# Routing weights written by accumulating scatters, and an expert product with its operands swapped, in a one-core mixer and expert layer

## The chip, the cores and the metric

The kernel runs as one program on one of the eight cores of a Trainium2 chip. The metric is the device time of one execution in microseconds, the median of several executions. A core has five engines that run their own instruction streams in order and meet at semaphores: TensorE (PE; its weight loads are shown apart as PEld), VectorE (DVE), ScalarE (ACT), GpSimd (POOL) and SyncE (SP). DMAs are issued by SP, ACT and POOL and are moved by the core's 16 DMA engines.

## The reference, cut to what matters

320 tokens of width 2048 (256 of a prompt, 64 of a sample) go through a mixing layer and then through a product-key expert layer. The change is in the second:

```python
q = (xb @ w_query).reshape(tb, 8, 2, 128)
s = einsum('thpc,hpkc->thpk', q, sub_keys)          # 128 keys in each half
s1, i1 = top_k(s[:, :, 0], 16)
s2, i2 = top_k(s[:, :, 1], 16)
cand_s = s1[..., :, None] + s2[..., None, :]         # 256 candidates
top_s, top_j = top_k(cand_s, 16)                     # eidx = 128 * i1 + i2 of them
g = softmax(top_s)
a = gelu(einsum('td,thkd->thk', xb, expert_u[eidx]))
out = einsum('thk,thkd->td', g * a, expert_v[eidx])  # 16384 experts, 8 x 16 a token
```

So each token has 128 pairs of an expert number and a weight `g`. All is in float32.

## The kernel before, in words

**The stream.** All weights pass through one stream of halves. A half is 512 KB, a tile [128, 1024], loaded by SP into one of LA = 5 `raw` buffers. `split_one` makes of it two float32r tiles: ACT copies it to `hi`, DVE subtracts, `lo = raw - hi`. Four `hi` and four `lo` buffers stand ready, so that the split is at most four halves ahead of PE. For a half, PE runs 8 blocks of 3 matmuls (hi by hi, hi by lo, lo by hi), 24 in all.

**The order** is written by `Plan`, a model of the engines' clocks that runs while the kernel is built. Tasks are generators; `step()` between two blocks of PE's work lets each task emit its next instructions when the model's clock of PE has come to the time at which its inputs are ready. Costs in this model (`pe_cost`, `dve_cost`, `pool_cost`, and 1.05 for a gather on POOL) set where an instruction stands in its engine's queue. On the chip each engine then takes its queue in that order and waits for what is late.

**The stages.** The mixing layer and the query product use 280 halves. Then come 256 halves of `Up` (128 tiles of experts; one expert tile is two halves, and it gives `hs = gelu(x U)` for 128 experts and 256 prompt tokens) and 256 halves of `Down`. The prompt's tokens meet all 16384 experts densely; the weights `g` are put into a table `gd` in DRAM, 128 x 128 experts by 256 tokens, with zeros where a token did not pick the expert. The order of groups of 4 tiles (`GE = 4`): 24 groups of Up, which are 192 halves; then the first Down; after it 8 Up tiles and one Down in turn; Downs alone at the end. `NSPILL = 20` groups of `hs` go through DRAM (`hd`).

**The table of weights.** `route_lane` finds the top 16 on DVE, `decode(i)` turns the results of token tile i into expert numbers and weights and marks `("dec", i)`. When the three tiles are decoded, `weights_lane` runs 64 times `g_unit` for four tokens each: DVE writes two one-hot tiles `oa` and `ob` by comparing with a row of numbers, POOL multiplies `ob` by the high and the low part of the weights, PE multiplies `oa` by `ob` (4 matmuls of 256 columns), ACT copies the result from PSUM into `st`, DVE adds the low part to it, and each 16 tokens SP writes `st` to `gd`. When all 64 are done it marks `G`. Then `weights_in` loads `gg`, the weights of two groups; `weigh` multiplies `hs` by them tile by tile (`h4`, `g4`) and splits the product into `w`.

**Down.** The 128 x 128 blocks of expert_v (`hi`, `lo`) are PE's stationary operand, the 256 token columns of `w` move. The sum over 8 tiles is added to `x2`, which holds the residual with features on partitions, and the last of them goes out as `yT`.

**The sample's 64 tokens** do not go through the dense products. `gathers` has POOL gather their rows of expert_u (`pur`) and expert_v (`pvr`) by indirect DMA, 128 times 512 KB each, into NGS = 4 buffers `gs`; DVE takes a dot product with each row of the first (`dot`) and adds each row of the second by its weight (`axpy`).

Most instructions are recorded by a helper, so line 221 stands for all of them but the stream's matmuls (line 359); the tiles' names tell them apart.

Of the kernel before, what the change touches and what calls it, by code (L numbers as in the profile page):

```python
# [31 lines left out]
GE = 4  # L32
# [3 lines left out]
NGS = 4  # L36
HSN = 4
RATE = 380e3
# [4 lines left out]
TB = 16  # L43
LA = 5
SA = 3

# [34 lines left out]

class Task:
# [4 lines left out]
class Plan:  # L87
# [4 lines left out]
    def __init__(self):  # L92
        self.clk = {e: 0.0 for e in ("pe", "act", "dve", "pool", "dma")}
        self.task = self.main = Task(None)
        self.tasks = []
        self.done = {}
        self.uses = {}
        self.table = None

# [37 lines left out]
    def move(self, queue, out, src):  # L137

        at = max(self.last(out, True), self.last(src, False))
        if queue != "sync":  # L140
            at = self.clk[queue] = max(self.clk[queue], at) + (1.0 if queue == "pool" else 0.1)
        n = size(out) * out.shape[0] * 4
        self.clk["dma"] = max(self.clk["dma"], at) + n / RATE
        self.touch(out, self.clk["dma"] + 2.0, True)
        self.touch(src, self.clk["dma"] + 2.0, False)

    def gather(self, out, idx):
        at = self.clk["pool"] = max(self.clk["pool"], self.last(out, True), self.last(idx, False)) + 1.05
        self.clk["dma"] = max(self.clk["dma"], at) + size(out) * out.shape[0] * 4 / RATE
        self.touch(out, self.clk["dma"] + GLAT, True)  # L150
# [6 lines left out]
    def spawn(self, gen):  # L157
        self.tasks.append(Task(gen, self.task.at))
# [53 lines left out]
class Engine:  # L212
# [4 lines left out]
    def __getattr__(self, op):  # L217
        f = getattr(self.eng, op)

        def call(*a, **k):  # L220
# [4 lines left out]
            if op == "indirect_dma_start":  # L225
                p.gather(out, k["in_offset"].ap)
                return r
# [22 lines left out]
def dve_cost(op, a, k):  # L250
# [3 lines left out]
    return 0.07 + n / 0.96e3 * (6.2 if op == "reciprocal" else 1)  # L254
# [12 lines left out]
def hybrid_kernel(ctx: ExitStack, tc: tile.TileContext, ins, outs, stop=None):  # L267
# [20 lines left out]
    RAW = Slots(plan, stream, "raw", [128, 1024], F32, LA)  # L288
    HI = Slots(plan, stream, "hi", [128, 1024], F32R, SA + 1)
    LO = Slots(plan, stream, "lo", [128, 1024], F32R, SA + 1)  # L290
# [11 lines left out]
    pool.memset(one, 1.0)  # L302
    mhalf = consts.tile([128, 1], F32, name="mhalf")
# [5 lines left out]
    class Stream:  # L309
        def __init__(self):  # L310
            self.loads, self.halves = deque(), deque()

        def fetch(self):
            p, h = next(self.src, (None, 0))
            if p is None:
                return False
            raw = RAW.take()
            p.load(raw, h)
            self.loads.append((p, h, raw))
            return True  # L320

        def split_one(self):
            p, h, raw = self.loads.popleft()
            hi, lo = HI.take(), LO.take()
            act.activation(hi, raw, AF.Copy)
            dve.tensor_tensor(lo, raw, hi, op=ALU.subtract)
            RAW.give(raw)
            self.halves.append((p, h, hi, lo))

        def fill(self):  # L330
            while RAW.free and self.fetch():
                pass

        def ahead(self):
            self.fill()
            while HI.free and self.loads:
                if self.halves and plan.last(self.loads[0][2], False) > plan.now() + 1:
# [10 lines left out]
        def half(self):  # L348
            p, h, hi, lo = self.halves.popleft()
# [17 lines left out]
            HI.give(hi)  # L367
            LO.give(lo)
# [3 lines left out]
    class Piece:  # L372

        GAP = 0.0025
# [135 lines left out]

    s1 = ExitStack()
# [24 lines left out]
    def late_consts():  # L536
# [17 lines left out]
        dve.tensor_scalar(bgh, vec[:, V_BG:V_BG + 48], 0.5, None, op0=ALU.mult)  # L554

# [442 lines left out]
    spawn(late_consts())  # L998

# [131 lines left out]
    def open_route():  # L1131
# [5 lines left out]
        for n in ("iT0", "iT1", "wH", "wL"):  # L1137
            R[n] = p.tile([128, DN], F32R if n == "wH" else F32, name=n)
# [18 lines left out]
        spawn(weights_lane())  # L1157
# [19 lines left out]
    def rows_task():  # L1177
# [19 lines left out]
        dve.scalar_tensor_tensor(xs, x2s, r2[:, 3:4], xs, op0=ALU.mult, op1=ALU.mult)  # L1197

# [4 lines left out]
    def wq_in(h, p):  # L1203
        def go(ps):
# [9 lines left out]
            if p == 1:  # L1214
                plan.see(sk)
                yield
                for i in range(3):
# [66 lines left out]
    def weights_lane():  # L1284
        yield from need(*[("dec", i) for i in range(3)])
        rtmp.close()
        q = open_pool(gtmp, "gtmp")
        OA = Slots(plan, q, "oa", [128, 4, 128], F32R, 3)
        OB = Slots(plan, q, "ob", [128, 4, 2, 128], F32R, 3)
        ST = Slots(plan, q, "st", [128, 128, TB], F32, 2)  # L1290
        st = None
        for t0 in range(0, DN, 4):
            if t0 % TB == 0:
                st, = yield from take(ST)
            oa, ob = yield from take(OA, OB)
            spawn(g_unit(t0, oa, ob, OA, OB, ST, st))
        while len(gdone) < DN // 4:
            yield
        gtmp.close()
        open_late()  # L1300
        mark("G")

    gdone = []
    gd = dram.tile([DN // TB, 128, 132 * TB], F32, name="gd")
    hd = dram.tile([NG, 128, GE * DN], F32, name="hd")

    def decode(i):
# [37 lines left out]
        rows = slice(0, 128) if i < 2 else slice(64, 64 + DN - TP)  # L1345
        n = rows.stop - rows.start
        if n:
            bk, = yield from take(BK)
            for a, nm in enumerate(("i0", "i1", "wt")):
                pe.transpose(bk[:, a * 128:a * 128 + n], R[nm][rows, i].rearrange("p h k -> p (h k)"), ident[rows, rows])  # L1350
            yield
            c = slice(i * 128, i * 128 + n)
            for a, nm in enumerate(("iT0", "iT1", "wH")):
                act.activation(R[nm][:, c], bk[:, a * 128:a * 128 + n], AF.Copy)
            dve.tensor_tensor(R["wL"][:, c], bk[:, 256:256 + n], R["wH"][:, c], op=ALU.subtract)
            BK.give(bk)
# [24 lines left out]
    def g_unit(t0, oa, ob, OA, OB, ST, st):  # L1381

        io = cst[:, None, C_IO:C_IO + 128].to_broadcast([128, 4, 128])
        col = lambda nm: R[nm][:, t0:t0 + 4, None].to_broadcast([128, 4, 128])
# [4 lines left out]
        yield  # L1389
        b2 = yield from take(BK, BK)  # L1390
        for k in range(4):
            mm(b2[k // 2][:, (k % 2) * 256:(k % 2) * 256 + 256], oa[:, k, :], ob[:, k].rearrange("p j i -> p (j i)"),
               start=True, stop=True)
        OA.give(oa)
        OB.give(ob)
        yield
        o, work = t0 % TB, []
        for a, bk in enumerate(b2):
            v = bk.rearrange("p (t j i) -> p t j i", t=2, j=2)
            s2 = st[:, :, o + 2 * a:o + 2 * a + 2].rearrange("p i t -> p t i")  # L1400
            act.activation(s2, v[:, :, 0], AF.Copy)
            work.append((s2, v[:, :, 1], bk))
        yield
        for s2, x, bk in work:
            dve.tensor_tensor(s2, s2, x, op=ALU.add)
            BK.give(bk)
        if o == TB - 4:
            plan.see(st)
            yield
            sync.dma_start(gd[t0 // TB][:, :128 * TB], st.rearrange("p i t -> p (i t)"))  # L1410
            ST.give(st)
        gdone.append(t0)

# [3 lines left out]
    def open_experts():  # L1417
# [3 lines left out]
        X["GS"] = Slots(plan, p, "gs", [128, W], F32, NGS)  # L1421
        spawn(gathers())

    def open_late():
        p = open_pool(late, "late")
        X["WT"] = Slots(plan, p, "w", [128, 2, 2 * GE, DN], F32R, 2)
        X["GG"] = Slots(plan, p, "gg", [128, DN // TB, 2 * GE * TB], F32, 1)

    def gathers():

        yield from need(("dec", 2))
        for src, use in (("pur", dot), ("pvr", axpy)):
            for j in range(128):
# [3 lines left out]
                spawn(use(j, gs))  # L1437
# [28 lines left out]
    class Up(Piece):  # L1466
# [16 lines left out]
        def after(self, b):  # L1483
            if b == 15:
                spawn(up_in(self.e, self.ps))

# [29 lines left out]
    def weigh():  # L1516
        for g in ORDER:
# [5 lines left out]
            h4 = hs.rearrange("p e (b t) -> p e b t", t=TB)  # L1523
            g4 = gg.rearrange("p b (e t) -> p e b t", t=TB)
            for k in range(GE + 1):
                if k < GE:
                    dve.tensor_tensor(h4[:, k], h4[:, k], g4[:, o + k], op=ALU.mult)
                    act.activation(w[:, 0, o + k, :], hs[:, k, :], AF.Copy)
                if k:
                    dve.tensor_tensor(w[:, 1, o + k - 1, :], hs[:, k - 1, :], w[:, 0, o + k - 1, :], op=ALU.subtract)  # L1530
                yield 0
# [14 lines left out]
    class Down(Piece):  # L1546

        def __init__(self, q, c, last):
            self.q, self.c, self.final, self.src = q, c, last, ins["pv"][8 * q + c]

        def ready(self, h):
            return plan.has(("w", self.q)) and MM.ready(1, plan.now())

        def begin(self, h):
            self.ps = MM.take()

        def moved(self, b):
            w, e = w_of[self.q], b % 8
            return self.ps[:, :DN], w[:, 0, e, :], w[:, 1, e, :], e == 0, e == 7

        def after(self, b):
            if b % 8 == 7:
                k = 2 * self.c + b // 8
                dve.tensor_tensor(x2[:, k, :DN], x2[:, k, :DN], self.ps[:, :DN], op=ALU.add)
                MM.give(self.ps)
                if self.final:
                    sync.dma_start(outs["yT"][k], x2[:, k, :DN])
            if b == 15 and self.c == 7:
                X["WT"].give(w_of.pop(self.q))
# [170 lines left out]
```

## Time and profile before

| | |
|---|---|
| time, median of 3 runs | 2733.84 us (2730.56 to 2739.34) |
| the profiled execution | 2734.69 us, span 2732.9 us from the first to the last instruction |
| PE busy | 2633.5 us, 96% of the span |
| DVE, ACT, POOL busy | 2024.8, 1137.6, 941.2 us |
| mean granted clock of TensorE | 0.985 |
| moved by DMA | 626.31 MB, 229 GB/s over the span |

The profile is one execution. Busy time is a mean over stages with different limits, so the stages are read one by one; PE's clock is given as a share of 2.4 GHz.

### The profile page before, as it was taken

Reading aid. Unit: us, or ns where it says so; the run is one execution under the profiler, and the core shown is the slowest. Engines: PE = TensorE matmul, PEld = TensorE weight load, DVE = VectorE, ACT = ScalarE, POOL = GpSimd, SP = SyncE. Lnnn points to the kernel's source line nnn. Section 1 sums busy time; section 2 is a strip of 40 time slices with the busy share of each in tenths; the row PEclk is TensorE's granted clock in tenths of the full one; section 3 lists DMA queues with packets and bytes.
Section 4 is the critical chain, followed back from the end, with each engine's and each line's share of the span. In section 5 each row is a group of like instructions: output and inputs, shape, how many; then the busy total and the mean of one; then the engine's idle time right before and its main releaser. Section 6 shows DMA issues by size and latency. Waiting matters only on the chain. (4 is left out here: it accounts for less than half of the span.)

```text
span 2732.9 us, 49761 instructions
## 1 busy us (share of the span) xinstructions
PE 2633.5 (96%) x19824; PEld 2587.2 (95%) x19824; DVE 2024.8 (74%) x3201; ACT 1137.6 (42%) x1613; POOL 941.2 (34%) x728
## 2 busy tenths in 40 slices
PE   7999999999999999999889898999999999999998
PEld 5899989999999999999889898999999999999997
DVE  8545666344444449999999998888778888888887
ACT  4344444333333334344444444444444444344442
POOL 7423342000001222045878877422223321122122
PEclk9999999999999999999999999999999999999999
DMA  7433333444444554456777787798988888888887
GB/s 229 166 124 120 123 113 131 150 151 147 154 147 147 176 173 141 152 185 222 271 279 275 272 284 271 296 318 302 333 310 308 310 329 298 310 299 312 289 293 255
DMA packets 217560, 626.31 MB, mean 229 GB/s; under 512 B 19824, under 2 KB 74096, under 8 KB 215280
## 3 DMA queue, kind: packets, MB, share of 16 engines
q1 hardware_dynamic: 174944, 470.40, 49.1%
q0 software_dynamic: 39504, 142.24, 14.9%
q10 hardware_dynamic: 2880, 10.49, 1.0%
q8 instruction: 157, 2.57, 0.4%
q14 instruction: 75, 0.61, 0.1%
HBM read 589.36 MB, written 33.69 MB: 228 GB/s over the span
## 5 line engine op out<-in xcount | busy, mean ns | idle before, releaser
L221 DVE TENSOR_TENSOR lo<-raw,hi 128x1024 fp32r<-128x1024 f32 x792 | 1035.7, 1311 | 568.3 <-ACT hi L221 560.8
L221 ACT ACTIVATE hi<-raw 128x1024 fp32r<-128x1024 f32 x792 | 835.0, 1058 | 1106.1 <-PE mm L359 961.0
L359 PE MATMUL mm<-xb,hi 128*128 128x256 f32 x4096 | 758.6, 287 | 2.9 <-ACT hs L221 2.8
L359 PE MATMUL mm<-w,hi 128*128 128x256 f32 x4096 | 737.6, 283 | 0.0
L359 PEld LDWEIGHTS mm<-xb,hi 128*128 128x128 f32 x4096 | 654.4, 196 | 3.3 <-ACT hs L221 3.0
L359 PEld LDWEIGHTS mm<-w,hi 128*128 128x128 f32 x4096 | 639.0, 192 | 0.0
L359 PE MATMUL mm<-x_g,hi 128*128 128x320 f32 x2688 | 602.9, 313 | 0.0
L359 PE MATMUL mm<-xb,lo 128*128 128x256 f32 x2048 | 587.9, 287 | 0.8 <-DVE lo L221 0.8
L359 PE MATMUL mm<-w,lo 128*128 128x256 f32 x2048 | 579.6, 283 | 0.0
L359 PEld LDWEIGHTS mm<-x_g,hi 128*128 128x128 f32 x2688 | 447.2, 188 | 8.0 <-issue 3.9
L359 PE MATMUL mm<-x_g,lo 128*128 128x320 f32 x1344 | 415.7, 309 | 0.9 <-DVE lo L221 0.9
L359 PEld LDWEIGHTS mm<-xb,lo 128*128 128x128 f32 x2048 | 402.2, 196 | 1.3 <-DVE lo L221 1.2
L359 PEld LDWEIGHTS mm<-w,lo 128*128 128x128 f32 x2048 | 393.2, 192 | 0.0
L221 POOL DMA_INDIRECT gs<-pvr,idx x128 | 178.6, 1395 | 531.3 <-DVE x2s L221 525.4
L221 POOL DMA_INDIRECT gs<-pur,idx x128 | 188.9, 1476 | 223.0 <-DVE gs L221 199.6
L359 PEld LDWEIGHTS mm<-x_g,lo 128*128 128x128 f32 x1344 | 252.7, 188 | 1.2 <-DVE lo L221 1.2
L221 POOL TENSOR_TENSOR r<-r 128x320 f32<-128x320 f32 (+2 forms) x39 | 39.6, 1017 | 403.0 <-DVE r L221 398.4
L221 DVE SCALAR_TENSOR_TENSOR gs<-gs,xs 128x1024 f32<-128x1024 f32 x128 | 173.1, 1355 | 0.1
L221 DVE SCALAR_TENSOR_TENSOR x2s<-gs,act,x2s 128x1024 f32<-128x1024 f32 x128 | 163.7, 1279 | 1.8 <-DMA gs<-pvr,idx 1.5
L221 POOL TENSOR_TENSOR ob<-ob,wL 128x512 fp32r<-128x512 f32 x64 | 142.3, 2223 | 5.0
L221 DVE TENSOR_TENSOR r<-r,mm 128x256 f32<-128x256 f32 x256 | 106.3, 415 | 43.5 <-PE mm L359 43.4
L221 POOL TENSOR_TENSOR ob<-ob,wH 128x512 fp32r<-128x512 f32 x64 | 114.8, 1794 | 62.2 <-DVE ob L221 56.7
(246 smaller groups left out, 2730.3 us busy)
## 6 DMA issues: line engine op xcount, KB each, us to landing
raw<-pu SPq DMA_DIRECT2D x256, 512.0 KB
raw<-pv SPq DMA_DIRECT2D x256, 512.0 KB
raw<-win SPq DMA_DIRECT2D x168, 512.0 KB
raw<-wbr SPq DMA_DIRECT2D x32, 512.0 KB
raw<-wout SPq DMA_DIRECT2D x32, 512.0 KB
raw<-wq SPq DMA_DIRECT2D x32, 512.0 KB
gd<-st SPq DMA_DIRECT2D x16, 1024.0 KB
gg<-gd SPq DMA_DIRECT2D x16, 1024.0 KB
```

The source lines that it names most:

```text
L221: r = f(*a, **k)
L359: nc.tensor.matmul(o, stays, moves, start=first, stop=last and n == len(products) - 1)
```

## The change

**Weights.** The one-hot products, `g_unit`, `weights_lane`, their pool and the buffers `st` go. The table is now two DRAM tensors `gd[0]`, `gd[1]`, one for each 128 prompt tokens. A new task `clear` has ACT fill them with zeros early, 32 DMAs of 512 KB. `decode(i)` works out for each pair of token and choice the word's place in the table (`ga`) and its weight (`gw`); `scatters` has POOL issue, for each of the 128 choices and both token tiles, one indirect DMA that adds 128 single words (one for each token) to the table. The sixteen of a head and tile may be in flight together; the first of the next head waits until the sixteen before it in that tile have landed. When the last 32 are issued, `G` is marked, and the first load of `gg` waits for their landing. Token tiles are now scored in the order 2, 0, 1, so that the sample's tile is decoded first.

**Down.** `w` (128 of the tokens) is stationary, 512 features of expert_v move. A half of Down is now 1 MB, two `raw` slots, read as 2 KB pieces. The result has tokens on partitions, so the residual is turned first (`turn`: 32 transposes on PE into `x2t`) and the sum is turned back at the end (`home`: 32 transposes). The tile `r1`, free after `turn`, now holds the gather buffers, five of them.

**The rest.** `weigh` takes a group of 4 tiles by one instruction each (1024 elements instead of 256). `raw`, `hi`, `lo` are rings of which two neighbours can be taken at once (LA = 4; two more `raw` slots when the expert stage opens, four more `hi` and `lo` after the last Up). The planner's costs are other numbers, and it books DMAs by queue.

```diff
-TB = 16
-LA = 5
+LA = 4
 SA = 3
+AHEAD = 6.0
...
+    def scatter(self, idx, src):
+        at = self.clk["pool"] = max(self.clk["pool"], self.last(src, False), self.last(idx, False)) + 1.05
...
-    return max(0.107, n + 0.003) if op == "matmul" else 0.216
+    return max(0.107, n + 0.0133) if op == "matmul" else 0.216
...
-    return 0.07 + n / 0.96e3 * (6.2 if op == "reciprocal" else 1)
+    return 0.16 + n / 0.96e3 * (6.2 if op == "reciprocal" else 1)
...
+    def clear():
+        yield from need(("x",))
+        for q in range(NG // 2):
+            for g in gd:
+                act.dma_start(g[q].rearrange("p (a x) -> p a x", x=128), zeros[:, None, :].to_broadcast([128, 2 * GE, 128]))
+            at = plan.now() + 12.0
+            while plan.now() < at:
+                yield
...
-                for i in range(3):
+                for i in (2, 0, 1):
...
+    def scatters():
+        yield from need(*[("ga", i) for i in range(DN // 128)])
+        for h in range(8):
+            for k in range(16):
+                for i in range(DN // 128):
+                    own = rounds.setdefault((h, i), [])
+                    j = 16 * h + k
+                    r = pool.indirect_dma_start(
+                        out=gd[i].rearrange("q p (x o) -> (q p x) o", o=1),
+                        out_offset=bass.IndirectOffsetOnAxis(ap=R["ga"][:, i, j:j + 1], axis=0),
+                        in_=R["gw"][:, i, j:j + 1], in_offset=None, compute_op=ALU.add)
+                    earlier = rounds[h - 1, i] if k == 0 and h else []
+                    after(r, earlier)
...
+                yield 0
...
-    def g_unit(t0, oa, ob, OA, OB, ST, st):
...
-        dve.tensor_tensor(ob[:, :, 1, :], io, col("iT1"), op=ALU.is_equal)
-        pool.tensor_tensor(ob[:, :, 0, :], ob[:, :, 1, :], col("wH"), op=ALU.mult)
-        pool.tensor_tensor(ob[:, :, 1, :], ob[:, :, 1, :], col("wL"), op=ALU.mult)
-        dve.tensor_tensor(oa, io, col("iT0"), op=ALU.is_equal)
...
-            act.activation(s2, v[:, :, 0], AF.Copy)
...
-            dve.tensor_tensor(s2, s2, x, op=ALU.add)
...
-        X["GS"] = Slots(plan, p, "gs", [128, W], F32, NGS)
+        x2t.append(p.tile([128, DN // 128, 2048], F32, name="x2t"))
+        X["GS"] = Slots(plan, None, "", None, None, NGS)
+        X["GS"].make = lambda i: r1[:, W * i:W * i + W]
+        RAW.extend(p.tile([128, 2048], F32, name="raw2"))
...
-            sync.dma_start(gg, gd[:, :, GE * TB * g:GE * TB * (g + 2)].rearrange("b p e -> p b e"))
+            for i in range(DN // 128):
+                r = sync.dma_start(gg[:, i].rearrange("p e t -> p (e t)"), gd[i][g // 2])
+                if g == ORDER[0]:
+                    after(r, rounds[7, i])
...
+            dve.tensor_tensor(h4, h4, gg[:, :, o:o + GE].rearrange("p i e t -> p e i t"), op=ALU.mult)
+            yield
+            act.activation(wh, hw, AF.Copy)
+            yield
+            dve.tensor_tensor(wl, hw, wh, op=ALU.subtract)
...
+        def block(self, b, hi, lo):
+            w, e, t = w_of[self.q], b // 2, b % 2
+            wh, wl = (w[:, i, e, 128 * t:128 * t + 128] for i in range(2))
+            vh, vl = (x.rearrange("p (k e d) -> p e k d", k=4, e=GE)[:, e % GE] for x in (hi, lo))
+            return (self.sums[t].rearrange("p (k d) -> p k d", k=4), e == 2 * GE - 1,
+                    ((wh, vh, e == 0), (wh, vl, False), (wl, vh, False)))
...
+            dve.tensor_tensor(x2t[0][:, t, c], x2t[0][:, t, c], ps, op=ALU.add)
```

Two places of the built programs show how instructions moved. First POOL's queue from the first gather on, before: `gs` are the gather buffers, `ob` the one-hot tiles, `wH` and `wL` the weights.

```order
L221 DMA gs_12688<-pur,idx 128x1024
L221 TENSOR_TENSOR ob_12677<-ob_12677,wH 128x4x128
L221 TENSOR_TENSOR ob_12677<-ob_12677,wL 128x4x128
L221 TENSOR_TENSOR ob_12679<-ob_12679,wH 128x4x128
L221 TENSOR_TENSOR ob_12679<-ob_12679,wL 128x4x128
```

POOL's queue of the change, where the scatters begin (`gd_92` and `gd_93` are the two tables, `r_80` the gather buffers):

```order
L271 DMA r_80<-pur,idx 128x1024 x4
L271 COPY gw<-wt 128x128
L271 DMA r_80<-pur,idx 128x1024
L271 DMA gd_92<-gw,ga 2097152x1
L271 DMA gd_93<-gw,ga 2097152x1
```

The 128 pairs of multiplications are gone. In their place stand 256 scatters, which alternate between the tables; 17 gathers stand ahead of the first of them, 8 between them, and 103 of `pur` and all 128 of `pvr` behind the last.

Second DVE's queue around the first `weigh`. Before (`lo` are the splits of the stream, the instructions on `gs,dots` are `dot`, those on `hs` the first `weigh`):

```order
L221 TENSOR_TENSOR lo_18127<-raw_17955,hi_18126 128x1024
L221 TENSOR_TENSOR lo_18159<-raw_17990,hi_18158 128x1024
L221 SCALAR_TENSOR_TENSOR gs_18014,dots<-gs_18014,xs 128x1024
L221 TENSOR_TENSOR lo_18193<-raw_18023,hi_18192 128x1024
L221 TENSOR_TENSOR hs_17576<-hs_17576,gg_18038 128x256 x2
L221 TENSOR_TENSOR w_18244<-hs_17576,w_18244 128x256
```

DVE's queue of the change at the same task (`r_80,dots` is `dot`; in the whole program 449 splits stand ahead of the first `dot` shown here, and 349 ahead of the last input of the first scatter):

```order
L271 TENSOR_TENSOR lo<-raw,hi 128x1024 x3
L271 SCALAR_TENSOR_TENSOR r_80,dots<-r_80,xs 128x1024
L271 TENSOR_TENSOR lo<-raw,hi 128x1024
L271 SCALAR_TENSOR_TENSOR r_80,dots<-r_80,xs 128x1024 x2
L271 TENSOR_TENSOR lo<-raw_10066,hi 128x1024
L271 SCALAR_TENSOR_TENSOR r_80,dots<-r_80,xs 128x1024 x2
L271 TENSOR_TENSOR lo<-raw_10066,hi 128x1024
L271 TENSOR_TENSOR lo<-raw,hi 128x1024
L271 TENSOR_TENSOR hs_15432<-hs_15432,gg_15508 128x1024
```

The first `dot` shown uses the first gather that POOL issues after the last scatter. It stands 100 splits behind the start of the scatters, and all later splits stand behind it. The 8 dots whose gathers are issued between scatters stand among those 100 splits. The first `weigh` was 463 splits from the start and is 453.

On PE, a half of Down was 24 matmuls of 256 columns on 512 KB and is 24 of 512 columns on 1 MB; 128 such halves stand where 256 stood. In both programs 192 halves of Up stand ahead of the first Down, and 64 behind it; 45 of the 128 dots stand on DVE ahead of the first Down's split in the change, 83 behind it.

## Rows read from the trace of the kernel before

**Rows 1.** The page, the span in 40 equal slices: busy tenths of two engines and of the DMA engines.

```profile
PE   7999999999999999999889898999999999999998
DVE  8545666344444449999999998888778888888887
...
DMA  7433333444444554456777787798988888888887
```

**Rows 2.** Windows: stretch, length; busy us (xcount) of PE, PEld, DVE, ACT, POOL; PEclk, DMA, GB/s.

```profile
600.00:700.00 100.00, 100.00 (x684) 100.00 (x684) 47.28 (x56) 37.23 (x42) 7.03 (x8) 1.00 0.43 149
1129.00:1266.00 137.00, 132.08 (x1076) 131.60 (x1075) 127.31 (x293) 61.63 (x81) 44.67 (x28) 0.98 0.56 188
1266.00:1797.00 531.00, 484.13 (x3811) 477.68 (x3810) 489.64 (x588) 245.90 (x363) 395.53 (x212) 0.95 0.78 279
1797.00:2719.00 922.00, 922.00 (x7686) 922.00 (x7685) 754.64 (x1024) 383.87 (x467) 227.39 (x172) 1.00 0.86 307
1900.00:2000.00 100.00, 100.00 (x836) 100.00 (x835) 83.66 (x122) 41.96 (x51) 24.76 (x23) 1.00 0.88 317
```

**Rows 3.** Timeline of PE, first Up, first Down, last Down: start, us, matmul.

```profile
1129.06 0.41 PE L359 MATMUL mm<-xb,hi 128*128 128x256 f32 x2
...
1797.36 0.40 PE L359 MATMUL mm<-w,hi 128*128 128x256 f32 x2
...
2719.05 0.28 PE L359 MATMUL mm<-w,lo 128*128 128x256 f32 x1
```

**Rows 4.** Waits in 1266 to 1797: us in total, times, longest.

```profile
PEld bk L221 <- POOL ob L221: 33.6, 10, 5.1
```

**Rows 5.** Groups by form: count, busy us, mean ns, idle before and its releasers.

```profile
L221 POOL DMA_INDIRECT gs<-pur,idx x128 | 188.9, 1476 | 223.0 <-DVE gs L221 199.6 <-issue 9.0 <-DVE idx L221 7.6
...
L221 DVE SCALAR_TENSOR_TENSOR gs<-gs,xs 128x1024 f32<-128x1024 f32 x128 | 173.1, 1355 | 0.1
L221 DVE SCALAR_TENSOR_TENSOR x2s<-gs,act,x2s 128x1024 f32<-128x1024 f32 x128 | 163.7, 1279 | 1.8 <-DMA gs<-pvr,idx 1.5
...
L221 DVE TENSOR_TENSOR r<-r,mm 128x256 f32<-128x256 f32 x256 | 106.3, 415 | 43.5 <-PE mm L359 43.4
...
L221 DVE TENSOR_TENSOR hs<-hs,gg 128x256 f32<-128x256 f32 x128 | 51.8, 419 | 2.6 <-DMA gg<-gd 2.6
...
L221 PE MATMUL bk<-ob,oa 128*128 128x256 f32 x256 | 48.0, 309 | 46.0 <-POOL ob L221 31.4 <-DVE st L221 14.2
...
L221 DVE TENSOR_TENSOR r<-mm,rb_x 128x320 f32<-128x320 f32 x56 | 27.1, 484 | 0.0
...
L221 PE MATMUL bk<-cst,r 128*128 128x128 f32 x20 | 2.8, 273 | 0.0
```

**Rows 6.** Timeline of POOL, gathers one behind the other: start, us.

```profile
2014.63 0.95 POOL L221 DMA_INDIRECT gs<-pvr,idx  x1 [0.30 <-issue]
2015.89 0.95 POOL L221 DMA_INDIRECT gs<-pvr,idx  x1 [0.30 <-issue]
2017.14 0.95 POOL L221 DMA_INDIRECT gs<-pvr,idx  x1 [0.30 <-DVE r L221]
```

**Rows 7.** Timeline of DVE over the same stretch.

```profile
2014.74 1.23 DVE L221 TENSOR_TENSOR lo<-raw,hi 128x1024 fp32r<-128x1024 f32 x1 [0.55 <-ACT hi L221]
...
2017.62 1.23 DVE L221 TENSOR_TENSOR lo<-raw,hi 128x1024 fp32r<-128x1024 f32 x1 [0.55 <-ACT hi L221]
```

**Rows 8.** Timeline of POOL, gathers while DVE is full.

```profile
1315.64 1.94 POOL L221 DMA_INDIRECT gs<-pur,idx  x1 [0.30 <-issue]
1317.89 0.95 POOL L221 DMA_INDIRECT gs<-pur,idx  x1 [0.30 <-issue]
```

**Rows 9.** The tile kT, a direct DMA of 128 rows issued by POOL: ns min/median/max.

```profile
L221 POOL DMA_DIRECT2D kT<-qk x8: 551/598/648, 228.5 to 441.4; - x8
```

**Rows 10.** Timeline of all engines at the end: the last gather and its use.

```profile
2721.25 1.87 POOL L221 DMA_INDIRECT gs<-pvr,idx  x1 [4.81 <-DVE x2s L221]
...
2726.49 1.28 DVE L221 SCALAR_TENSOR_TENSOR x2s<-gs,act,x2s 128x1024 f32<-128x1024 f32 x1 [1.55 <-DMA gs<-pvr,idx]
```

More of the change, by code (lines that the diff above doesn't have):

```diff
@@ L79, in give, with __init__, extend, left @@
         self.free.sort()
+class Ring:
+    def __init__(self, plan, tile_, n):
+        self.plan = plan
+        self.at = [tile_[:, i, :] for i in range(n)]
+        self.both = [tile_[:, i:i + 2, :].rearrange("p s c -> p (s c)") for i in range(n - 1)] + [None]
+        self.slots = Slots(plan, None, "", None, None, n)
+        self.slots.make = lambda i: self.at[i]
+    def extend(self, *pairs):
+        for x in pairs:
+            self.slots.free += [(self.plan.now(), len(self.at) + i) for i in range(2)]
+            self.at += [x[:, :1024], x[:, 1024:]]
+            self.both += [x, None]
+        self.slots.free.sort()
+    def left(self):
+        return len(self.slots.free)
+    def take(self, n):
+        at = sorted(i for t, i in self.slots.free[:n])
+        assert at[-1] - at[0] == n - 1
+        parts = [self.slots.take() for _ in range(n)]
+        return self.both[at[0]] if n == 2 else parts[0], parts
+    def give(self, parts):
+        for x in parts:
+            self.slots.give(x)
 class Task:
@@ L225, in call @@
             if op == "indirect_dma_start":
-                p.gather(out, k["in_offset"].ap)
+                if k["in_offset"] is None:
+                    p.scatter(k["out_offset"].ap, k["in_"])
+                else:
+                    p.gather(out, k["in_offset"].ap)
                 return r
@@ L335, in ahead @@
             self.fill()
-            while HI.free and self.loads:
-                if self.halves and plan.last(self.loads[0][2], False) > plan.now() + 1:
+            while self.loads and HI.left() >= self.loads[0][0].SLOTS:
+                if self.halves and max(plan.last(self.loads[0][2], False), plan.clk["dve"] - AHEAD) > plan.now() + 1:
                     break
@@ L508, in row_norm @@
         yield
+    gd = [dram.tile([NG // 2, 128, 2 * GE * 128], F32, name=f"gd{i}") for i in range(DN // 128)]
     s1 = ExitStack()
@@ L1282, in route_lane, with late_lane, after @@
                     spawn(decode(i))
-    def weights_lane():
+    def late_lane():
         yield from need(*[("dec", i) for i in range(3)])
         rtmp.close()
[L1287 to L1297, printed above, removed]
+        open_late()
+    rounds = {}
+    def scatters():
[11 more added lines that the diff above has]
+                    after(r, earlier)
+                    tc.declare_no_dep(r.ins, group=f"tile{i}", reason="other words", keep=[x.ins for x in earlier])
+                    own.append(r)
+                    tc.add_to_no_dep_group(f"tile{i}", r.ins)
+                yield 0
+        at = plan.clk["pool"] + 5.0
+        while plan.now() < at:
             yield
-        gtmp.close()
-        open_late()
         mark("G")
-    gdone = []
-    gd = dram.tile([DN // TB, 128, 132 * TB], F32, name="gd")
+    def after(r, others):
+        for x in others:
+            tc.add_manual_dep(r.ins, x.ins.name, mybir.DependencyInfo(mybir.DependencyClass.Sync, mybir.DependencyReason.DATA),
+                              reason="adds to the same words")
     hd = dram.tile([NG, 128, GE * DN], F32, name="hd")
@@ L1546, in hybrid_kernel, with load @@
     class Down(Piece):
+        SLOTS = 2
         def __init__(self, q, c, last):
-            self.q, self.c, self.final, self.src = q, c, last, ins["pv"][8 * q + c]
+            self.q, self.c, self.final = q, c, last
+        def load(self, raw, h):
+            n = 8 * self.q + 2 * self.c
+            sync.dma_start(raw.rearrange("p (k x) -> p k x", k=4),
+                           ins["pv"][n:n + 2, :, :, 512 * h:512 * h + 512].rearrange("n k p x -> p (n k) x"))
         def ready(self, h):
-            return plan.has(("w", self.q)) and MM.ready(1, plan.now())
+            return plan.has(("w", self.q)) and (h == 1 or MM.ready(2, plan.now()))
@@ L1554, in begin @@
         def begin(self, h):
[L1555 to L1559, printed above, removed]
-        def after(self, b):
[L1562 to L1565, printed above, removed]
-                if self.final:
-                    sync.dma_start(outs["yT"][k], x2[:, k, :DN])
-            if b == 15 and self.c == 7:
-                X["WT"].give(w_of.pop(self.q))
+            if h == 0:
+                self.sums = [MM.take(), MM.take()]
@@ L1575, in down @@
     def down(q, last=False):
-        for c in range(8):
+        for c in range(4):
             yield Down(q, c, last)
```

191 lines of the change are left out of this document (114 added, 77 removed).

## The prediction

> **What bounds the kernel now.** I read the page's slices first, then TensorE by stage, then the waits of the one stage where it is not full, then single instructions.
>
> The slices [rows 1] show PE at nine tenths or more nearly everywhere; the eights stand in the second half of the route and of the table of weights, and there DVE is full too. The stages [rows 2] put figures to it. From 1900 to 2000 us PE does 836 matmuls of 256 columns in 100 us, 119.6 ns each, at full granted clock; from 600 to 700 it does 684 of 320 columns, 146.2 ns each. The difference, 26.6 ns for 64 columns, is 0.416 ns a column, which is the 2.4 GHz level; what is left, 119.6 - 256 x 0.416 = 13.1 ns, is a price for each matmul. From 1797 to 2719 the same pace holds with DVE busy 754.6 of 922 us: this stage is bound by PE alone. From 1266 to 1797, where the table of weights is made, 3811 matmuls at 119.6 ns would take 455.8 us and took 531: 75.2 us are lost, with DVE busy 489.6 us of 531 and the granted clock at 0.95 instead of 1.00. What PE waits for there is the chain of `g_unit`, POOL's products first of all [rows 4]. From 1129 to 1266 (1076 matmuls, 128.7 us of work) 8.3 us are lost with DVE at 93%.
>
> First Up at 1129.06, first Down at 1797.36, last matmul at 2719.05 [rows 3]; the span ends 13.9 us later. I sum against the profiled execution, 2734.7 us, which lies 0.9 us above the median.
>
> **The change, part by part.**
>
> *Fewer matmuls.* The 256 of `g_unit` [rows 5] go: 256 x 119.6 ns = -30.6 us. Down does 3072 matmuls of 512 columns instead of 6144 of 256. No row has a pace for 512 columns; by the two above it is 119.6 + 256 x 0.416 = 226 ns, so 694.3 us instead of 734.8: -40.5 us. The bounds are 2 x 119.6 ns (nothing gained) and 213 ns (no fixed price, 40 us more); the line through two lengths is the nearest. The Trainium skill, TensorE: Matmul & The Clock Gate, section Back-to-back issue gap, has a fixed part of only 2.5 ns, which would make 215.8 ns and the sum 31 us lower; by the same rule 256 columns would take 109 ns, and the rows here say 119.6, so the trace decides.
>
> *The stall of the old table.* Its DVE work (two one-hot tiles, two sums), its POOL products and its PSUM copies go, and with them what waited: -75.2 us. Whether something new waits there comes next.
>
> *New on PE:* 64 transposes of 128 x 128. Nearest is the 273 ns of a 128-column matmul in float32 [rows 5], a latency and so an upper bound; +16 us (0 to 17).
>
> *The route's end.* The decodes of tiles 0 and 1 and 17 dots now stand between splits 328 and 349 of the stream. That DVE work (21 splits, 12 of the dots, 13 comparisons and reductions, some small ones: about 64 us with 1.23 us for a split, a comparison or a reduction, 1.355 for a dot [rows 5, 7] and 0.25, an estimate, for each small one) meets 60 us of PE: +5 us.
>
> *The scatters.* No row shows one. All 256 stand in POOL's queue between the last input `ga` (349 splits done) and the gather for the dot behind split 449. At PE's pace 100 splits are 100 x 24 x 119.6 ns = 287 us. In that time POOL must issue 256 scatters and 9 gathers. The planner that wrote the order booked 1.05 us for each. Gathers issued one behind the other start 1.25 to 1.26 us apart, 0.95 us of work and 0.30 us of issue [rows 6], and that with a split on DVE each 2.88 us [rows 7], which is just the load that DVE has beside the scatters. So 265 x 1.26 = 334 us. The first scatter of each head waits for the landing of the last of the head before; the last gather of all was in use 3.4 us after its issue ended [rows 10], less one scatter issued meanwhile, 2.1 us, seven times: 15 us. Then the landing of the gather that the dot wants, 3.4 us: 352 in all, 65 us more than PE needs. What is queued behind: the dot stands in DVE's queue ahead of all later splits, so DVE stops, `lo` tiles run out after at most three halves (8.6 us), and PE stops. The eight dots among the 100 splits spread this stop over the stage. So 65 - 8.6 = +57 us. SP's first `gg` waits for the same landings, with the later `raw` loads behind it; it is late together with DVE and costs nothing more.
>
> The bounds: a direct DMA of 128 rows takes POOL 0.60 us [rows 9], with 0.30 of issue 0.9 us each, and the stop is 0. With DVE full, gathers start 2.25 us apart [rows 8]: 265 x 0.99 = 262 us more, +319. I take 1.26 us, because instruction and DVE's load are nearest there; a scatter builds 128 addresses as a gather does. That the words are added in DRAM has no row; it lies behind POOL's issue and shows only in the waits between heads.
>
> The Trainium skill bears on the price, SBUF — State Buffer, section Who interferes with whom: a DVE instruction with two inputs from SBUF shuts out a GpSimd instruction that reads SBUF until it is done. Each split has two such inputs. The rows agree where DVE is full and not where it only splits; by the rule alone each scatter that meets a split would lose up to 1 us, and the sum would go toward the first rival below.
>
> *Down's margin.* After the first Down DVE has 64 splits at 1.23 us, 128 of double length (2.3 us, by 0.42 us at 256 elements and 1.23 at 1024), 83 dots at 1.355, 128 axpys at 1.279, 56 long instructions of `weigh` at 1.23 (before, 0.42 each at a quarter of the length), 128 sums of 512 columns at 0.69 us (by 0.415 at 256 and 0.484 at 320) [rows 5, 7]: 805 us beside 878 us of PE, 92%. DVE at 82% cost PE nothing and at 93% 6% [rows 2]. Downs have only two pairs of `hi` and `lo` until the Ups end, so one pair is made while the other is used, 5.4 us. Bounds 0 and 53 us; +18, since the 93% stand in a stage of short chained instructions.
>
> *Hidden.* The zeros are written early by DMAs from ACT's queue, where the DMA engines are three to four tenths busy [rows 1]; uncovered, 16.8 MB at 307 GB/s [rows 2] would be 55 us. The loads of expert_v come in 2 KB pieces, at a DMA share of 0.86 [rows 2]; Down's data per column are unchanged.
>
> The sum: 2734.7 - 30.6 - 40.5 - 75.2 + 16 + 5 + 57 + 18 = **2685 us**, 1.8% below the median.
>
> **The rivals.**
>
> *A: scatters cost more than 1.45 us (slower).* Place: POOL between splits 349 and 449. Each 0.1 us is 26.5 us, so the 49 us that the forecast gains are gone at 1.45 us. The mean gather of `pur`, 1.476 us [rows 5], with 0.30 of issue is 1.78: 265 x 0.52 = 138 more, 2823 us. For it: DVE's splits do meet POOL, and the addition in DRAM may want more addresses or land late. Against it: [rows 6, 7]; while DVE waits for a dot it does not disturb POOL.
>
> *B: scatters at the planner's pace or below (1.05 us or less).* Less data than a gather of 4 KB rows; the direct DMA speaks for it. The stop vanishes: 2685 - 57 = 2628 us.
>
> *C: 512 columns gain nothing*, if the fixed price grows with length: 2725 us. For it: no row at 512. Against: 256 and 320 lie on the 2.4 GHz slope.
>
> *D: DVE becomes the bound in Down* as from 1129 to 1266: 53 instead of 18 us, 2720 us. For it: 92%. Against: 82% cost nothing for 922 us.
>
> **How the numbers follow.** Forecast 0.40 (own range 2660 to 2715), B 0.20, C and D together 0.12, A 0.28. A measurement here tells 0.3% (8 us) from no change. Faster: the forecast, B, and half of C and D, 0.66; within 0.3%: the edge between C, D and A, 0.07; slower: A less that edge, 0.27. For 8 in 10 the range reaches from 2615 (B with a little of the stalls gone) to 2785 (half of A); above it lies 0.13, below it 0.06.
>
> **What would show it.** Matmuls of Down 226 ns apart; 24 of them in 5.4 us. Scatters starting about 1.26 us apart, with seven waits of a few us for DMA at the heads. Between first scatter and first `gg` DVE idle for gathers, PE idle for `lo`, some 57 us in all, and the granted clock below 1.00. The first Down at about 1129 + 551 + 5 + 57 + 10 = 1752 us instead of 1797. After it PE near 98%. Wrong: a scatter period far from 1.26 us, a gap at the heads near 10 us, or PE starved in Down.

## The result, and the profile after

The changed kernel takes 2899.41 us (median of 4 runs, 2897.74 to 2903.01) where the kernel before took 2736.59 us beside it: a ratio of 1.0599, 95% interval 1.0576 to 1.0623. It is 6% slower; 2685 us had been forecast. The profiled execution is one of 2899.26 us.

The page's slices, for the rows of [rows 1] and two more:

```profile
PE   7899999999999999999555725469999999999999
DVE  8446664444445578898122212158888888888895
POOL 6323330000002220157888888853444343333330
PEclk9899999999999999999777967779999999999999
DMA  7666433444444545568555545389999998999984
```

From slice 20 to 26, PE is half empty, DVE nearly idle, and POOL at eight tenths. Nothing else in the program looks worse than before. The stages, as in [rows 2]:

```profile
1129.00:1344.00 215.00, 208.29 (x1716) 206.89 (x1716) 192.49 (x473) 97.08 (x123) 77.53 (x53) 0.99 0.64 222
1344.00:1898.70 554.70, 307.02 (x2421) 305.18 (x2420) 134.10 (x126) 121.13 (x153) 468.72 (x264) 0.78 0.52 117
1945.00:2480.00 535.00, 534.42 (x3169) 472.15 (x3169) 442.83 (x442) 211.51 (x184) 204.69 (x138) 1.00 0.94 343
2480.00:2897.00 417.00, 407.18 (x1744) 326.48 (x1743) 337.71 (x256) 152.47 (x94) 125.61 (x77) 0.99 0.84 309
2700.00:2800.00 100.00, 100.00 (x431) 80.49 (x430) 84.20 (x67) 35.92 (x22) 34.55 (x23) 1.00 0.94 351
```

The second row is the stage of the scatters: 2421 matmuls of 119.6 ns are 289.6 us of work, and it lasts 554.7 us. Of the 265 us between, 17 are matmuls at a lower granted clock (0.78 in this stage, 307.0 us busy), the others idle time. Its waits (engine, line, waited for: us in all, times, longest) and the groups of the two instructions concerned, for [rows 4, 5]:

```profile
DVE r L271 <- DMA r<-pur,idx: 247.9, 8, 76.3
PEld mm L416 <- DVE lo L271: 196.5, 8, 69.4
PE mm L416 <- DVE lo L271: 194.8, 8, 69.2
...
POOL gd L271 <- issue: 77.0, 250, 1.1
POOL gd L271 <- DMA gd<-gw,ga: 6.7, 6, 2.9
```

```profile
L271 POOL DMA_INDIRECT gd<-gw,ga x256 | 460.6, 1799 | 83.7 <-issue 77.0 <-DMA gd<-gw,ga 6.7
...
L271 DVE SCALAR_TENSOR_TENSOR r<-r,xs 128x1024 f32<-128x1024 f32 x128 | 158.1, 1254 | 319.0 <-DMA r<-pur,idx 319.0
```

The chain reads from the bottom up: POOL issues scatters with nothing but 0.30 us of issue between them; eight dots in DVE's queue wait for gathers that stand among the scatters, 248 us; the splits behind them are late, and PE waits for `lo`, eight times. The landing of the words in DRAM hardly counts (6.7 us). The first Down starts at 1977.23 us instead of 1797.36 [rows 3]:

```profile
1977.23 0.40 PE L416 MATMUL mm<-hi,w 128*128 128x512 f32 x1
```

A scatter is 1799 ns on average, but few are near that. Two places of POOL's timeline (start, us), the first beside the DVE instructions that ran there, the second where DVE waited from 1638.9 to 1715.2 us for a gather:

```profile
1350.60 1.98 POOL L271 DMA_INDIRECT gd<-gw,ga  x1 [0.30 <-issue]
1352.89 1.98 POOL L271 DMA_INDIRECT gd<-gw,ga  x1 [0.30 <-issue]
...
1651.74 1.55 POOL L271 DMA_INDIRECT gd<-gw,ga  x1 [0.30 <-issue]
1653.60 1.55 POOL L271 DMA_INDIRECT gd<-gw,ga  x1 [0.30 <-issue]
```

```profile
1348.81 2.35 DVE L271 TENSOR_TENSOR lo<-raw,hi 128x1024 fp32r<-128x1024 f32 x2
1351.08 1.21 DVE L271 SCALAR_TENSOR_TENSOR r<-r,xs 128x1024 f32<-128x1024 f32 x1
...
1637.64 1.23 DVE L271 TENSOR_TENSOR lo<-raw,hi 128x1024 fp32r<-128x1024 f32 x1 [1.65 <-ACT hi L271]
1715.21 1.23 DVE L271 SCALAR_TENSOR_TENSOR r<-r,xs 128x1024 f32<-128x1024 f32 x1 [76.34 <-DMA r<-pur,idx]
```

Sorted by whether a long DVE instruction ran meanwhile, the 148 scatters that met none all took 1.55 to 1.57 us. Of those that met one split and no other long instruction, the 12 that start ahead of it took 1.55 us. Of the 67 that start within it, 66 ended 1.42 us after the split: 2.58 us for a start 0.07 us into it, 1.70 us at 0.95. The last one started 0.06 us before the split's end and took 1.55. Even alone a scatter is 0.60 us longer than a gather [rows 6], and this is the larger part.

### The profile page after: what moved, and what is told of

Read it like the earlier page. It is cut to its first block, busy times and chain, and to the rows that moved or that the text cites. A ratio compares the mean times of both kernels' runs of the same rounds, so it can differ in the third digit from the quotient of the medians.

```text
span 2897.6 us, 41477 instructions
## 1 busy us (share of the span) xinstructions
PE 2589.5 (89%) x16554; PEld 2403.6 (83%) x16554; DVE 1774.6 (61%) x2509; ACT 1042.1 (36%) x1274; POOL 1161.1 (40%) x858
## 5 line engine op out<-in xcount | busy, mean ns | idle before, releaser
L271 DVE TENSOR_TENSOR lo<-raw,hi 128x1024 fp32r<-128x1024 f32 (+1 forms) x616 | 868.1, 1415 | 628.9 <-ACT hi L271 628.7
L271 ACT ACTIVATE hi<-raw 128x1024 fp32r<-128x1024 f32 (+1 forms) x616 | 719.0, 1170 | 1363.7 <-PE mm L416 1130.0
L271 POOL DMA_INDIRECT gd<-gw,ga x256 | 460.6, 1799 | 83.7 <-issue 77.0
L416 PE MATMUL mm<-hi,w 128*128 128x512 f32 x1280 | 408.7, 396 | 0.0
L271 POOL DMA_INDIRECT r<-pvr,idx x128 | 206.9, 1617 | 348.6 <-DVE x2s L271 336.9
L416 PEld LDWEIGHTS mm<-hi,w 128*128 128x128 f32 x1280 | 241.3, 189 | 57.9
L416 PE MATMUL mm<-xb,w 128*128 128x512 f32 x1152 | 275.7, 398 | 2.8 <-DVE xb L271 2.7
L271 POOL DMA_INDIRECT r<-pur,idx x128 | 176.8, 1381 | 225.1 <-DVE r L271 208.5
L416 PEld LDWEIGHTS mm<-xb,w 128*128 128x128 f32 x1152 | 217.1, 189 | 55.9 <-DVE xb L271 3.6
L416 PE MATMUL mm<-lo,w 128*128 128x512 f32 x640 | 254.0, 397 | 2.8 <-DVE lo L271 2.8
```

Source lines behind the costliest of these rows:

```text
L271: r = f(*a, **k)
L416: nc.tensor.matmul(o, stays, moves, start=first, stop=last and n == len(products) - 1)
```

## The experiments

The theory, **PRICE**: the loss is POOL's time for 256 scatters, 1.55 us each plus 0.30 of issue plus a wait for DVE's splits, 2.09 us a DMA over the stage (554.7 us by 265), and it holds whatever the order. Rivals: **ORDER** (the eight dots among the splits stop DVE; placed elsewhere they would not), the landing of the words, or another part of the change. A time without a ratio is of one execution.

### The planner is told the true price

```diff
-        at = self.clk["pool"] = max(...) + 1.05
+        at = self.clk["pool"] = max(...) + 2.1
```

> Only the planner's price of a scatter is changed, from 1.05 to 2.1 us; the same instructions are issued, the dots stand later in VectorE's queue. Theory PRICE (the loss is 256 scatters at about 2.1 us on GpSimd, and nothing that needs the table can start before): the first Down stays near 1977 us and the time within 2870 to 2920 us; TensorE is then full for longer and idle in one piece before the first Down. Rival ORDER (the loss comes from the eight dots that stand among the splits and stop VectorE): the splits run on, the stage takes about 353 us, the first Down comes near 1750 and the time near 2690 us.

Measured: 2877.52 us, ratio 1.0519 (1.0502 to 1.0537); first Down at 1945.8 us, last scatter at 1931.5. Windows of this kernel, while PE has Up to do, and from there to the first Down:

```profile
1344.00:1697.00 353.00, 335.71 (x2763) 335.10 (x2762) 153.21 (x138) 137.50 (x173) 304.83 (x140) 0.98 0.73 206
1697.00:1945.00 248.00, 27.84 (x219) 27.43 (x217) 14.04 (x11) 11.85 (x14) 201.38 (x129) 0.56 0.31 40
```

PE is now fed for 353 us and then stands for most of 248, as PRICE has it. The first Down comes 31 us earlier than the 1977 us of PRICE: in the change PE still had 69 us of Up's matmuls to do behind the last scatter. ORDER falls: the order is worth 22 of the 163 us. And the scatters did not get on better while PE ran: POOL's and DVE's timelines of this kernel, at one time:

```profile
1600.42 2.57 POOL L271 DMA_INDIRECT gd<-gw,ga  x1 [0.30 <-issue]
1603.30 2.58 POOL L271 DMA_INDIRECT gd<-gw,ga  x1 [0.30 <-issue]
1606.18 2.58 POOL L271 DMA_INDIRECT gd<-gw,ga  x1 [0.31 <-issue]
```

```profile
1600.35 1.23 DVE L271 TENSOR_TENSOR lo<-raw,hi 128x1024 fp32r<-128x1024 f32 x1 [1.66 <-ACT hi L271]
1603.23 1.23 DVE L271 TENSOR_TENSOR lo<-raw,hi 128x1024 fp32r<-128x1024 f32 x1 [1.66 <-ACT hi L271]
1606.11 1.23 DVE L271 TENSOR_TENSOR lo<-raw,hi 128x1024 fp32r<-128x1024 f32 x1 [1.65 <-ACT hi L271]
```

Each scatter starts 0.07 us into a split and takes 1.03 us more than alone. With the 0.30 of issue it lasts 2.88 us, exactly a split's period, so the next one starts at the same place of the next split: one scatter for each split, for as long as the splits run on.

### Is it the split's two inputs from SBUF?

```diff
+                X["PS"] = BK.take()
+                pe.transpose(X["PS"][:, 0:128], ident, ident)
...
-            dve.tensor_tensor(lo, raw, hi, op=ALU.subtract)
+            dve.tensor_tensor(v(lo), v(raw), X["PS"][:, None, 0:128].to_broadcast([128, 8, 128]), op=ALU.subtract)
```

> As the first experiment (planner's scatter price 2.1 us), but from the end of the route on the 512 KB splits subtract a tile in PSUM instead of hi (so the low parts are not the reference's): the same length of instruction, with one input from SBUF instead of two. Theory PORT (a scatter waits for a VectorE instruction that has two SBUF inputs): beside such splits a scatter keeps its 1.55 us, the period is near 1.87 us throughout, the last scatter starts near 1345 + 490 = 1835 us instead of 1931, the time is about 2780 us. Rival BUSY (any VectorE instruction or the stream's other traffic slows a scatter): the period stays at 2.88 us beside splits, the time at 2860 to 2890 us.

Measured: 2784.74 us; last scatter at 1840.9 us. The same two timelines, of this kernel:

```profile
1600.96 1.55 POOL L271 DMA_INDIRECT gd<-gw,ga  x1 [0.30 <-issue]
1602.81 1.55 POOL L271 DMA_INDIRECT gd<-gw,ga  x1 [0.30 <-issue]
1604.66 1.55 POOL L271 DMA_INDIRECT gd<-gw,ga  x1 [0.30 <-issue]
```

```profile
1602.02 1.22 DVE L271 TENSOR_TENSOR lo<-raw,bk 128x1024 fp32r<-128x1024 f32 x1 [1.66 <-PE mm L423]
1604.90 1.22 DVE L271 TENSOR_TENSOR lo<-raw,bk 128x1024 fp32r<-128x1024 f32 x1 [1.66 <-PE mm L423]
```

The splits are as long and as frequent, and more scatters meet one (176 of 256, against 122 in the first experiment); yet 247 of the 256 take under 1.60 us. The other nine all start within a dot or a split that still subtracts `hi`, and both have two inputs from SBUF. So it is not a busy DVE that delays a scatter, but a DVE instruction with two inputs from SBUF: 93 us between this run and the first experiment. The Trainium skill, SBUF — State Buffer, section Who interferes with whom, states this of a GpSimd instruction that reads SBUF, and the trace agrees. For a DMA the section tells of a probe in which a `tensor_tensor` stalled none; here it does, and the measurement decides. A split with the right values and one input from SBUF was not tried.

### More of PE's work ahead of the first Down

```diff
-NSPILL = 20
+NSPILL = 30
```

> Planner's scatter price 2.1 us as in the first experiment, and all 256 halves of Up stand ahead of the first Down instead of 192 (NSPILL 30 instead of 20; ten more groups go through DRAM). Theory LOCK (beside an unhindered split every 2.88 us only one scatter is issued, so giving TensorE work slows the scatters): 187 scatters or gathers while TensorE runs, the last 78 alone at 1.85 us, the last scatter near 2025 us, first Down near 2040, time 2770 to 2850 us. Rival (the scatters keep their mean of 2.17 us): last scatter near 1920 us, first Down near 1935, time 2680 to 2740 us.

Measured: 2865.58 us; last scatter at 2000.9 us, first Down at 2019.2.

```profile
1344.00:1882.00 538.00, 488.66 (x3999) 487.85 (x3998) 217.00 (x193) 199.06 (x250) 464.19 (x213) 0.95 0.74 195
...
2019.00:2863.80 844.80, 727.35 (x3106) 583.69 (x3106) 708.11 (x644) 273.54 (x166) 334.29 (x224) 0.93 0.91 331
2752.60:2863.80 111.20, 0.03 (x1) 0.00 (x0) 82.68 (x65) 0.60 (x1) 77.87 (x60) 0.51 0.87 301
```

LOCK holds for the stage, with 2.57 us from scatter to scatter on average. The total is 16 us above the range: PE is idle 117 of the last 845 us, which the expectation had not counted. The third row shows where: 111 us of them lie behind PE's last work, while POOL and DVE still gather and add rows of expert_v for the sample. These rows come behind the dots, which end at 2486 us here and at 2272 us in the change; in Down itself, reloads included, PE is idle 6 us.

### What a scatter's own price is made of

Without the addition:

```diff
-                        in_=R["gw"][:, i, j:j + 1], in_offset=None, compute_op=ALU.add)
+                        in_=R["gw"][:, i, j:j + 1], in_offset=None)
```

> The scatters write the word instead of adding to it (where two choices of a token name the same expert, one weight is lost); same count, same order. Theory PRICE (GpSimd's own work for 128 addresses, and VectorE beside it): the undisturbed scatter stays at 1.55 us and the time within 2880 to 2920 us. Rival ADD (the accumulation makes the instruction dear): the undisturbed scatter falls to the 0.95 us of an undisturbed gather, the mean period to some 1.4 us, and the time to 2690 to 2760 us.

Half the words:

```diff
-                        out_offset=bass.IndirectOffsetOnAxis(ap=R["ga"][:, i, j:j + 1], axis=0),
-                        in_=R["gw"][:, i, j:j + 1], in_offset=None, compute_op=ALU.add)
+                        out_offset=bass.IndirectOffsetOnAxis(ap=R["ga"][:64, i, j:j + 1], axis=0),
+                        in_=R["gw"][:64, i, j:j + 1], in_offset=None, compute_op=ALU.add)
```

> Each scatter adds 64 words instead of 128 (the weights of half the prompt tokens are left out); same count, same order. Theory ADDRESS (the price is mostly for each address): the undisturbed scatter falls from 1.55 to 0.8 to 1.0 us, the mean period to about 1.4 us, the time to 2700 to 2760 us. Rival FIXED (the price is mostly for each instruction): 1.4 us or more undisturbed, time 2840 us or more.

Measured: 2920.11 us and 2838.18 us. The rows of the scatters, plain writes first, 64 words second (ns min/median/max, first and last start):

```profile
L271 POOL DMA_INDIRECT gd<-gw,ga x256: 962/967/1982, 1344.4 to 1701.0; - x128
```

```profile
L271 POOL DMA_INDIRECT gd<-gw,ga x256: 1403/1416/2372, 1344.7 to 1834.5; - x128
```

The addition costs 0.58 us of POOL's own time an instruction (1548 against 967 ns), so ADD is right on POOL's price and PRICE, which held that it stays at 1.55 us, is not; that the time came out at the end of PRICE's range has another reason, told below. Halving the words saves 0.13 us of 1.55: the price is mostly the instruction's, not the address's (FIXED, whose time of 2840 us is missed by 2). Of the 65 us that POOL is busy less there, 34 are these 0.13 us, the rest shorter waits for splits.

But the plain writes, done at 1702 us instead of 1898, made nothing faster. PE's timeline of that kernel:

```profile
1601.23 0.37 PE L416 MATMUL mm<-xb,hi 128*128 128x256 f32 x1 [2.43 <-issue]
1604.03 0.37 PE L416 MATMUL mm<-xb,hi 128*128 128x256 f32 x1 [2.43 <-issue]
1606.83 0.37 PE L416 MATMUL mm<-xb,lo 128*128 128x256 f32 x1 [2.43 <-issue]
```

From about 1470 us on, PE starts a matmul only each 2.1 to 4.2 us, mostly 2.8, and the profile shows nothing that it waits for. This sets in by degrees from 1435 us and lasts until 1727, 25 us beyond the last write. So the writes were spaced:

```diff
+                    for _ in range(3):
+                        nc.gpsimd.memset(zeros, 0.0)
```

> Plain writes as in the second experiment (a doubly chosen expert keeps one weight), each followed by three small memsets on GpSimd, which space them to about 1.9 us. Theory RATE (128 words written every 1.27 us overrun what the writes land at, and TensorE's issue suffers): with the slower pace TensorE runs at 120 ns a matmul between its waits, time 2850 to 2900 us. Rival WRITE (it is the plain write itself): TensorE again starts a matmul only each 2 to 3 us while scatters are issued, time 2920 us or more.

Measured: 2913.55 us, with 2.23 us from scatter to scatter. The same 190 us in both kernels, plain writes back to back and then spaced:

```profile
1500.00:1690.00 190.00, 25.33 (x68) 19.61 (x68) 3.68 (x3) 3.93 (x5) 142.97 (x148) 0.50 0.08 20
```

```profile
1500.00:1690.00 190.00, 104.83 (x840) 104.43 (x840) 44.63 (x39) 41.68 (x52) 162.28 (x337) 0.78 0.37 117
```

68 matmuls against 840: it is the pace of the writes (RATE), not the write. The time lies above its range; the spaced scatters met splits and came 2.23 and not 1.9 us apart. By what way writes 1.27 us apart hold up PE is not shown and stays open: the DMA engines were busy 0.08 of that stretch, so RATE's reason, writes that overrun their landing, is not shown either.

### Half the scatters, and none

```diff
-        for h in range(8):
+        for h in range(4):
```

> Only four of the eight heads are scattered (128 instead of 256 scatters; half the weights are left out). The planner then puts the next dots behind 402 splits instead of 449. Theory PRICE: 134 DMAs of about 2.1 us against 53 splits of TensorE's work (152 us) stop the stage by some 120 us instead of 265, so the time is 2740 to 2780 us. Rival (the loss is not proportional to the count, but comes from the landing or the first gg): 2850 us or more.

The second has range(0).

> No scatter is issued (the table stays zero, so the experts' part for the prompt tokens is left out); the rest of the change stands, the dots move forward into the freed time. Theory PRICE (the scatters are the only thing that the change loses by): the sum of the prediction without its scatter term, 2628 us, 2610 to 2650. Rival (another part, Down or the moved dots, costs as well): 2660 us or more.

Measured: 2750.11 us and 2614.83 us. The stages of the kernel without scatters:

```profile
1129.00:1344.00 215.00, 208.27 (x1717) 206.88 (x1717) 192.47 (x472) 97.37 (x124) 77.56 (x53) 0.99 0.67 224
1344.00:1699.00 355.00, 355.00 (x2960) 355.00 (x2960) 266.17 (x320) 148.84 (x185) 107.05 (x95) 1.00 0.95 351
1699.00:2240.00 541.00, 540.88 (x3067) 470.90 (x3066) 458.66 (x379) 214.62 (x178) 215.10 (x139) 1.00 0.94 343
```

From 1344 to the first Down at 1699 PE is full. The loss goes with the count: 0, 135 and 285 us for none, 128 and 256 scatters. Taken together, the rest of the change is a gain: with no table made at all, 119 us on the kernel before. The zeros written early cost nothing that shows: the first Up starts at 1128.6 us here and at 1129.06 in the kernel before.

### The old table with the new Down

The one-hot products and `weights_lane` of before, with the rest of the change; 20 of the gathers may go ahead of the table's end:

```diff
             for j in range(128):
+                if src == "pur" and j == 20:
+                    yield from need(("G",))
                 gs, = yield from take(X["GS"])
```

> The old table (one-hot products) with the rest of the change: 512 columns, turned residual, weigh by groups, rings. 20 of the gathers are let go ahead of the table's end, the others wait for it. Theory (only the table was a loss): Up and table at most the 668 us of before, Down 920 us as in the change: 2690 to 2725 us. Rival (VectorE or the DMA engines become the bound in Down with more dots behind it): 2735 us or more.

Measured: 2705.45 us, ratio 0.989 (0.9874 to 0.9907): 1.1% faster than the kernel before, and faster than the change.

```profile
1266.00:1783.00 517.00, 478.37 (x3804) 474.02 (x3803) 441.51 (x493) 242.73 (x357) 312.74 (x173) 0.96 0.68 232
1783.00:2705.00 922.00, 897.99 (x4651) 769.47 (x4649) 775.81 (x705) 352.62 (x263) 335.72 (x223) 0.99 0.95 338
```

Down from its first matmul (1783.8) to the end takes 921.7 us where it took 935.5; the table's stage 14 us less than in [rows 2], with DVE less full. With 45 gathers let go instead of 20:

> As the seventh experiment, with 45 instead of 20 gathers let go ahead of the table's end. Theory DMA (Down's loss of some 20 us is its DMA engines at 0.96): 18 gathers fewer in Down give it back, 2690 to 2703 us. Rival TABLE (the dots cost the table's stage what they save in Down): 2705 us or more.

Measured: 2712.76 us, ratio 0.9916 (0.9898 to 0.9934). The intervals overlap. DMA's forecast did not come: Down takes 926.3 us in this kernel's profile, so the moved gathers gave nothing back there. The time fits TABLE, but its reason, a saving in Down, does not.

## Why the prediction was wrong, step by step

- **Scatters, +57 us: the step that failed.** Its mechanism held: POOL's queue between the last `ga` and the gather for the dot behind split 449, DVE stopped by dots, PE starved for `lo`; and so did its 287 us of PE's work (289.6). Its price did not: 1.26 us was taken from gathers [rows 6], and it was 2.09, the waits between heads included. By the prediction's own rule of 26.5 us for each 0.1 us this is +220 us, less the 15 us that it counted apart for those waits. Three parts of it: the scatter alone takes 1.55 and not 0.95 us, 256 x 0.60 = +154 us; its waits for DVE, 460.6 - 256 x 1.548 = +64 us; the waits between heads were 6.7 and not 15 us, -8. 2685 + 210 = 2895, against 2899.3 in the profile.
- **Why the price was wrong, twice.** It was said that the addition "lies behind POOL's issue"; the plain write shows 0.58 us of it on POOL. And [rows 6, 7] were read as gathers that a split does not disturb. They start ahead of a split or at its very end, where scatters are not disturbed either. In the trace of before, of the gathers that met one split and no other DVE instruction, 37 start ahead of it and take 0.95 to 0.99 us, one starts with it and takes 0.95, and three start 0.2 to 0.4 us into it and take 1.69 to 1.81. These three end 0.82 us after the split, as the scatters end 1.42 us after it. One in [rows 8] takes 1.94 us.
- **The rule that was weighed and set aside** told the right side, and no row spoke against it: the rows were of another phase. The Trainium skill, SBUF — State Buffer, section SBUF: two separate sides, says that the one that starts first has the port and the other waits. The scatters agree. The splits don't, and the measurement decides: in the trace of before, 129 splits start within a gather and meet nothing else on POOL, and all are 1.20 to 1.23 us long, as alone; so are the 22 in the change that start within a scatter and meet no other.
- **Rival A** is what came, beyond its 1.78 us and within the 2.25 us that the prediction had as a bound [rows 8]. What spoke against it, "while DVE waits for a dot it does not disturb POOL", is right, and is why the first experiment's scatters, with DVE at work, took longer still.
- **Fewer matmuls.** 431 in 100 us are 232.0 ns for 512 columns, forecast 226: +18 us, a little of rival C. The 30.6 us of `g_unit` and the 75.2 us of the old stall are gone (no scatters: PE full).
- **Transposes:** the matmul behind four of them starts 0.36 us after the first, so some 6 us for 64, forecast 16. **Route's end:** 1716 matmuls in 215 us are 9.8 us more than at 119.6 ns each; the forecast left the 8.3 us of before in place and added 5.
- **Down's margin:** PE is idle 0.6 + 9.8 us, 4 of them behind its last instruction; forecast 18. DVE is at 82% (780.5 of 952 us), not 92, and rival D did not come. From the first Down to the end it takes 920.3 us; the steps give 935.5 - 40.5 + 8 (half of the transposes) + 18 = 921. That these agree so well is luck: the matmuls took more than forecast, and the transposes, the idle time and the end behind PE's last instruction (4.6 us, before 13.5) took less.
- **Without the scatter term** the sum was 2628 us; the kernel without scatters took 2614.8. That is no clean test of the other terms, since 90 dots instead of 30 stand ahead of the first `weigh` there. (The terms of the sum as written add to 2684.4, not 2685.)

## What to carry to other kernels

A new instruction on a full queue needs its own price before its count is multiplied: here 256 times 0.83 us turned a forecast gain of 1.8% into a loss of 6%. When a row is to show that two engines do not disturb each other, look where in the other's instruction it starts, and take the rows of both phases. And a better order is no cure where the stage is short of an engine's time: giving PE its work slowed the scatters that it later waited for.

## What the runs showed of the hardware

- An indirect DMA that adds costs POOL 1.55 us for 128 words and 1.42 for 64, one that writes 0.97, a gather 0.95, with 0.30 of issue between them.
- An indirect DMA that starts within a DVE instruction with two SBUF inputs waits: it ends 1.42 us after that instruction if it adds, 0.82 us if it gathers. Beside one with an input from PSUM it does not wait. It falls into step with the splits: 2.57 + 0.30 us beside splits each 2.88.
- Plain indirect writes of 128 words each 1.27 us slowed PE to a matmul each 2.1 to 4.2 us without a wait in the profile, in one execution; at 2.23 us apart they did not.
- A matmul of 512 columns costs 18.7 ns over its columns at 2.4 GHz, one of 256 columns 12.9.
